# Updating the sample retention states in the feed-forward stage instead of the mixer

## The chip, the core and the metric

The kernel runs on one core of a Trainium2 chip. The core has several engines that work side by side and wait for each other by semaphores: PE (matrix products; PEld is its loading of stationary operands), DVE (elementwise, two operands), ACT (elementwise, one operand, with functions), POOL, and SP, which here only issues DMA transfers, in order. Times are microseconds (us) on the device. The metric is the time of one execution, the median over several runs.

## The reference

One decoder layer for 256 prompt positions and 8 samples of 8 new positions each (320 columns N in the kernel; D_MODEL is 2048). The inputs' norm feeds one projection, whose columns go to an S5 mixer (a diagonal state-space scan) and to retention with 8 heads of width 128. Their outputs are joined, projected and added; a SwiGLU feed-forward part (D_FF 5632) and a last norm follow. The part that the change touches is the state that retention hands back for the samples:

```
chunk = math.gcd(l, RET_CHUNK)                  # 8 for a sample: one chunk
k_decay = exp(log_gamma[:, None] * (chunk - 1.0 - idx))
r_new = r * chunk_decay + einsum('bhmd,bhme->bhde', kc * k_decay, vc)
```

For each of 8 heads and 8 samples `r_new` is a 128x128 matrix: the old one (input `state_ret`, in the kernel `r0[h]`, 512 KB per head) times a constant, plus the product of 8 decayed keys with 8 values. It is an output (`rs_o[h]`, 512 KB per head) and nothing later in the layer reads it. The old state is also read by the attention of the same head.

## The kernel before

The weights, some 210 MB, are streamed once. `wload` fetches tiles of 128x1024 (512 KB) on SP's queue into `raw`, ACT casts them to `hi` (fp32r, the one-pass format), and DVE forms the rest, `lo = raw - hi`. `gemm` then makes each product of a weight tile in three one-pass matmuls (L136 to L138: hi by hi, hi by lo, lo by hi) of 320 columns. The weights' tiles rotate through a pool `wp` with three buffers for each of `raw`, `hi` and `lo`. From the first `up` gemm of the feed-forward stage on, the loads use a second pool, `wp2`, with four, three and three.

The stages follow each other: up to 421 us the mixer (all columns of `w_in`, with the heads and the S5 chunks woven in), up to 563 us the output projections (`w_out`, `w_glu`, `w_out`), then the feed-forward stage: `ffn_in` with eleven pairs of gemms, gate and up, for each quarter of D_FF, and `ffn_out`.

PE's and POOL's orders are written by hand. A planner's clock `clk` adds an assumed cost for each matmul, and generators (`head_k`, `head_v`, the S5 chunks) yield delays from the table `DL`; when one is due, `run_due` puts its next burst of small matmuls between two matmul triples of the running gemm. DVE's, ACT's and SP's orders come from a scheduler with priorities. SP's queue is in order: a load whose buffer isn't free holds back all the loads behind it.

For each head, `do_q` loads `r0[h]` into `rt` (one buffer); `head_k` transposes the keys (`pst`), scales them (`kd`, ACT, L628) and makes the scores (`pss`); `head_v` does the values (`vT`), spreads the sample's values by a block mask over four samples (`vb`, POOL, L650), and makes the output `po`, reading `rt`. Last comes `update` (L707 to L717), due `DL["u"]` later. The keys and values of the samples lie at partitions 64 to 127, 32 of them for each group of four samples. The two products `psu` are plain fp32 matmuls with 32 rows of contraction and 512 columns, in the PSUM pair "misc", which `pst`, `pss`, `pk` and others share. DVE adds them to the old state in `rt` (scalar_tensor_tensor, shown under its helper's line L175), and SP stores `rt`.

At the feed-forward stage's entry, `hhi` and `hlo` of the last column block and the sum of squares `acc` (DVE) are completed; `ffn_norm` makes the reciprocal root: a matmul `ps_r` sums `acc`, a chain of 11 small DVE operations from `ms` to `ry` computes the root, and a second `ps_r` broadcasts it. ACT copies the result to `rbc2`, which the evictions of the gemms' results read.

Of the kernel before, what the change touches and what calls it, by code (L numbers as in the profile page):

```python
# [12 lines left out]
F32 = mybir.dt.float32  # L13
F32R = mybir.dt.float32r
# [3 lines left out]
ADD, SUB, MUL = ALU.add, ALU.subtract, ALU.mult  # L18
PSUM = bass.MemoryType.PSUM

P = 128
D = 2048
KT = D // P
NP, NB, NS = 256, 8, 8
N = NP + NB * NS
H = 8
# [18 lines left out]
def hybrid_kernel(ctx, tc, xT, w_in, w_out, w_glu, w_fi, w_fo, vecs, s5p, bc, x0,  # L45
# [3 lines left out]
    pe, act, dve, pool, sp = nc.tensor, nc.scalar, nc.vector, nc.gpsimd, nc.sync  # L49

    cst = ctx.enter_context(tc.tile_pool(name="cst", bufs=1))
    wp = ctx.enter_context(tc.tile_pool(name="wp", bufs=1))
    ps_acc = ctx.enter_context(tc.tile_pool(name="ps_acc", bufs=2, space=PSUM))

    def f(t):
        return t.bitcast(F32)
# [4 lines left out]
    ones = cst.tile([P, P], F32, name="ones")  # L61
    pool.memset(ones, 1.0)
    vec = cst.tile([P, vecs.shape[1]], F32, name="vec")
    voff = {}
    o = 0
    for nm, n in (("g_mix", 16), ("g_ffn", 16), ("g_fin", 16), ("d", 8), ("bglu", 8), ("gn", 8)):
# [7 lines left out]
    class Clk:  # L74
        now = 0.0
        n = 0
# [19 lines left out]
    def mm(cost, *a, **k):  # L96
        pe.matmul(*a, **k)
        clk.now += cost
# [71 lines left out]
    def tt(out, a, b, op):  # L170
        dve.tensor_tensor(out, a, b, op)  # L171
        return out

    def stt(out, a, s, b, o1, o2):
        dve.scalar_tensor_tensor(out, a, s, b, o1, o2)  # L175
        return out
# [48 lines left out]
    mp = retpool.enter_context(tc.tile_pool(name="mp", bufs=1, side="right"))  # L225
# [7 lines left out]
    def misc(name):  # L233
        return ps_m.tile([P, 512], F32, name=name, tag="misc", bufs=2)
# [4 lines left out]
    rtok = mp.tile([P, 3], F32, name="rtok")  # L239
    csr = mp.tile([P, 2, N], F32, name="csr")  # L240
    kdc = mp.tile([P, H, 3], F32, name="kdc")
    bmk = mp.tile([P, 4], F32, name="bmk")
    gqt = mp.tile([P, H, NS], F32, name="gqt")
    retp = mp.tile([P, H, N], F32, name="retp")

# [357 lines left out]
    GAM = [1.0 - 2.0 ** (-5.0 - h) for h in range(H)]  # L603
# [17 lines left out]
    def head_k(h, q_, qg, k_, R):  # L621
        yield DL["k"]
        pst = misc("pst")
        for i, s in enumerate(STARTS):
            tr(pst[:, P * i:P * i + P], k_[:, s:s + P])
        kd = mp.tile([P, 3, P], F32, name="kd", tag="kd", bufs=1)
        for i in range(3):
            act.mul(kd[:, i], pst[:, P * i:P * i + P], kdc[:, h, i:i + 1])  # L628
        pss = misc("pss")
        mm(0.43, pss[:, 0:256], k_[:, 0:P], q_[:, 0:256], start=True, stop=True)  # L630
        mm(0.22, pss[:, 256:384], k_[:, P:256], q_[:, P:256], start=True, stop=True)
        mm(0.22, pss[:, 384:448], k_[:, 192:320], q_[:, 256:320], start=True, stop=True)
        sm = mp.tile([P, 384], F32, name="sm", tag="sm", bufs=1)
        mk = R["mk"]
        tt(sm[:, 0:256], pss[:, 0:256], mk[:, 0:NP], MUL)
        tt(sm[:, 256:384], pss[:, 256:384], mk[:, 0:P], MUL)
        tt(smp[64:128, :, 0:NS], pss[64:128, 384:448].rearrange("p (b t) -> p b t", t=NS),
           mk[64:128, NP:320].rearrange("p (b t) -> p b t", t=NS), MUL)
        R["kd"], R["sm"] = kd, sm

    def head_v(h, v_, qg, rt, R):
        yield DL["v"]
        pst2 = misc("pst2")
        for i, s in enumerate(STARTS):
            tr(pst2[:, P * i:P * i + P], v_[:, s:s + P])
        vT = mp.tile([P, 3, P], F32, name="vT", tag="vT", bufs=1)
        for i in range(3):
            act.mul(vT[:, i], pst2[:, P * i:P * i + P], rtok[:, i:i + 1])
        vb = mp.tile([P, 4, P], F32, name="vb", tag="vb", bufs=1)
        pool.tensor_tensor(vb[64:128], vT[64:128, 2].unsqueeze(1).to_broadcast([64, 4, P]),  # L650
                           bmk[64:128].unsqueeze(2).to_broadcast([64, 4, P]), MUL)
        yield DL["o"]
        kd, sm = R["kd"], R["sm"]

        po = ps_v.tile([P, 4, P], F32, name="po", tag="po", bufs=1)
        mm(0.22, po[:, 0], sm[:, 0:P], vT[:, 0], start=True, stop=True)
        mm(0.22, po[:, 1], sm[:, P:256], vT[:, 0], start=True, stop=False)
        mm(0.22, po[:, 1], sm[:, 256:384], vT[:, 1], start=False, stop=True)

        for g in range(2):  # L660
            mm(0.22, po[:, 2 + g], smp[:, 4 * g:4 * g + 4].rearrange("p b t -> p (b t)"), vT[:, 2],
               start=g == 0, stop=False, skip_group_check=True)
        for g in range(2):
            for j in range(4):
                mm(0.06, po[32 * j:32 * j + 32, 2 + g], qg[:, 4 * g + j], rt[:, 4 * g + j], start=False,
                   stop=True, tile_position=(0, 32 * j), skip_group_check=True)
        st = mp.tile([P, 4, 6], F32, name="st", tag="st", bufs=1)
        mv = mp.tile([P, 2, 4], F32, name="mv", tag="mv", bufs=1)
        y = mp.tile([P, 2, 4], F32, name="gy", tag="gy", bufs=1)
        with tc.high_priority(offset=GN):  # L670
            for i in range(4):
                dve.bn_stats(st[:, i], po[:, i])
                dve.bn_aggr(mv[:, :, i], st[:, i])
            ts(mv[:, 1], mv[:, 1], -0.5, MUL, -0.5 * EPS, ADD)
            rsqrt(mv[:, 1], y[:, 0], y[:, 1])
            stt(y[:, 1], mv[:, 0], -1.0, y[:, 0], MUL, MUL)
        on = mp.tile([P, 4, P], F32, name="on", tag="on", bufs=1)
        for i in range(4):
            act.activation(on[:, i], po[:, i], AF.Identity, scale=y[:, 0, i:i + 1],
                           bias=y[:, 1, i:i + 1])  # L680
        psr = misc("psr")
        mm(0.22, psr[:, :P], kd[:, 0], vT[:, 0], start=True, stop=False)
        mm(0.22, psr[:, :P], kd[:, 1], vT[:, 1], start=False, stop=True)
        rp = mp.tile([P, P], F32, name="rp", tag="rp", bufs=1)
        act.copy(rp, psr[:, :P])
        sp.dma_start(rp_o[h], rp)
        yield DL["c"]
        pn = misc("pn")
        for i in range(4):
            tr(pn[:, P * i:P * i + P], on[:, i])  # L690
        pairs_ = ((pn[:, 0:NP], retp[:, h, 0:NP], slice(0, NP)),
                  (pn[:, NP:].rearrange("p (b t) -> p b t", t=32)[:, :, 0:NS],
                   retp[:, h, NP:].rearrange("p (b t) -> p b t", t=NS), slice(NP, N)))
        sg = R.get("sgt")
        for i_, o, sl in pairs_:
            if sg is None:
                act.mul(o, i_, v("gn", h))
            else:
                g_ = sg[:, sl]
                if sl.start:  # L700
                    g_ = g_.rearrange("p (b t) -> p b t", t=NS)
                stt(o, i_, v("gn", h), g_, MUL, MUL)
        R["gn"] = True
        if sg is not None:
            R["sg"] = True
        yield from update(h, kd, vb, rt)

    def update(h, kd, vb, rt):
        yield DL["u"]
        psu = [misc("psu") for _ in range(2)]  # L710
        for i in range(2):
            r = slice(64 + 32 * i, 96 + 32 * i)
            mm(0.43, psu[i], kd[r, 2], vb[r], start=True, stop=True, tile_position=(64 + 32 * i, 0))
        for i in range(2):
            rv = rt[:, 4 * i:4 * i + 4]
            stt(rv, rv, float(GAM[h] ** NS), psu[i].rearrange("p (b e) -> p b e", e=P), MUL, ADD)
        sp.dma_start(rs_o[h], rt)  # L717

    def proj(i):
        return gemm("ps_p", w_in[i], KT, xhi, xlo)  # L720
# [53 lines left out]
    def do_g(h):  # L774
        ps = proj(11 + 4 * h)
        sg = mp.tile([P, N], F32, name="sg", tag="sg", bufs=2)
        with tc.high_priority(offset=EVAC):
# [6 lines left out]
    DL = dict(b1=14.2, k1=2.2, b2=4.6, scan=15.6, x=2.2, k=5.5, v=6.1,  # L784
              o=2.2, u=6.0, c=10.0, n2=1.6, n2b=2.4, nm=7.8)
# [225 lines left out]
    def norm_ps(name):  # L1011
        return ps_n.tile([P, 512], F32, name=name, tag="n", bufs=2)

    def ffn_norm():
# [2 lines left out]
        yield DL["n2b"]  # L1017
        act.copy(rbc2, next(rg))

    def ffn_in(c):  # L1020
        ahi = fp.tile([P, FCT, N], F32R, name="ahi", tag="ahi", bufs=2)
        alo = fp.tile([P, FCT, N], F32R, name="alo", tag="alo", bufs=2)
        for i in range(FCT):
            n = c * FCT + i
            if n == 0:
                spawn(ffn_norm(), DL["n2"])
            pg = gemm("ps_fg", w_fi[2 * n], KT, hhi, hlo)
            g = fp.tile([P, N], F32, name="fg", tag="fg", bufs=2)
            tt(g, pg, rbc2, MUL)
            act.activation(g, g, AF.Silu)  # L1030
            if n == 0:
                wpool[:] = [wp2, WP2]
            pu = gemm("ps_fu", w_fi[2 * n + 1], KT, hhi, hlo)
            u = fp.tile([P, N], F32, name="fu", tag="fu", bufs=2)
            tt(u, pu, rbc2, MUL)
            tt(u, u, g, MUL)
            act.copy(ahi[:, i], u)
            tt(alo[:, i], u, f(ahi[:, i]), SUB)
        return ahi, alo

    wp2 = ctx.enter_context(tc.tile_pool(name="wp2", bufs=1, reuse_waits="tile"))
# [133 lines left out]
```

## Time and profile before

| | |
|---|---|
| runs | 1510.04, 1511.94, 1514.68 us; median 1511.94 |
| profiled execution | 1513.66 us, its span 1510.0 us |
| mean granted clock of PE | 0.987 |
| busy | PE 98%, DVE 57%, ACT 40%, POOL 5% |
| moved by DMA | 224.49 MB, 149 GB/s in the mean |

The span goes from the first to the last instruction on the core; the execution's own time is 3.7 us longer. The granted clock is the share of TensorE's full speed that the chip allowed; 0.5 is 1.2 GHz, 1.0 is 2.4 GHz. Idle time of an engine counts only where the engine that sets the end waits for it.

### The profile page before, as it was taken

How to read it: one execution, taken by the hardware profiler on the slowest of the kernel's cores; microseconds unless marked ns; L12 is line 12 of the kernel's file. 1: busy time of each engine (PE TensorE's matmuls, PEld its weight loads, DVE VectorE, ACT ScalarE, POOL GpSimd, SP SyncE). 2: the span in 40 equal slices, each digit the busy share in tenths (PEclk: the TensorE clock that was granted, in tenths of full speed). 3: DMA queues.
4: the chain of work that ended last, by engine and by line, in shares of the span. 5: the costliest groups of instructions: out<-in, count | busy, mean ns of one | idle time of the engine just before them, and what ended most of it. 6: DMA issues, size and time to landing. Idle time of an engine off the chain costs nothing.

```text
span 1510.0 us, 26190 instructions
## 1 busy us (share of the span) xinstructions
PE 1478.7 (98%) x10574; PEld 1450.5 (96%) x10574; DVE 864.6 (57%) x1490; ACT 608.9 (40%) x971; POOL 80.3 (5%) x167
## 2 busy tenths in 40 slices
PE   8989999999999999999999999999999999999997
PEld 8989899898999999999999999999999999999996
DVE  7988767776755675444454444444444444444454
ACT  6545445454434553333333333333333333333352
POOL 1331310300000000000000000000000000000001
PEclk9999999999999999999999999999999999999998
DMA  8344334333364444444444445544444544445443
GB/s 274 126 149 144 131 112 148 120 123 119 129 230 149 148 164 145 149 154 149 147 152 153 137 135 152 177 145 150 145 133 150 173 153 146 148 129 148 147 153 108
DMA packets 77832, 224.49 MB, mean 149 GB/s; under 512 B 14865, under 2 KB 27281, under 8 KB 77713
## 3 DMA queue, kind: packets, MB, share of 16 engines
q1 hardware_dynamic: 77568, 222.79, 45.6%
q8 instruction: 83, 1.36, 0.4%
q14 instruction: 37, 0.30, 0.1%
q10 hardware_dynamic: 144, 0.04, 0.0%
HBM read 213.85 MB, written 7.63 MB: 147 GB/s over the span
## 4 chain that ended last, share of the span: by engine, by line
PE 67%; DVE 0%; ACT 0%; DVEq 0%; issue 0%
PE ps_fg L136 7%; PE ps_fo L136 7%; PE ps_fo L137 7%; PE ps_fu L137 7%; PE ps_fg L137 7%; PE ps_fu L136 7%; PE ps_fg L138 7%; PE ps_fu L138 7%; PE ps_fo L138 7%; PE ps_o L137 1%; PE ps_o L138 1%; PE ps_o L136 1%; PE ps_g L137 1%; PE ps_g L138 1%; PE ps_g L136 1%; DVE x L171 0%
## 5 line engine op out<-in xcount | busy, mean ns | idle before, releaser
L126 DVE TENSOR_TENSOR lo<-raw,hi 128x1024 fp32r<-128x1024 f32 (+1 forms) x420 | 472.2, 1125 | 416.1 <-ACT hi L125 415.8
L125 ACT CAST hi<-raw 128x1024 fp32r<-128x1024 f32 (+1 forms) x420 | 406.4, 968 | 742.5 <-PE ps_fo L137 189.3
L136 PE MATMUL ps_fo<-ahi,hi 128*128 128x320 f32 x704 | 217.5, 309 | 0.0
L137 PE MATMUL ps_fo<-alo,hi 128*128 128x320 f32 x704 | 217.5, 309 | 0.0
L136 PE MATMUL ps_fg<-hhi,hi 128*128 128x320 f32 x704 | 217.5, 309 | 0.0
L138 PE MATMUL ps_fo<-ahi,lo 128*128 128x320 f32 x704 | 217.5, 309 | 0.0
L138 PE MATMUL ps_fg<-hhi,lo 128*128 128x320 f32 x704 | 217.4, 309 | 0.0
L137 PE MATMUL ps_fg<-hlo,hi 128*128 128x320 f32 x704 | 217.4, 309 | 0.0
L137 PE MATMUL ps_fu<-hlo,hi 128*128 128x320 f32 x704 | 217.4, 309 | 0.0
L136 PE MATMUL ps_fu<-hhi,hi 128*128 128x320 f32 x704 | 217.4, 309 | 0.0
L138 PE MATMUL ps_fu<-hhi,lo 128*128 128x320 f32 x704 | 217.4, 309 | 0.0
L136 PE MATMUL ps_p<-xhi,hi 128*128 128x320 f32 x576 | 187.8, 326 | 0.0
L137 PE MATMUL ps_p<-xlo,hi 128*128 128x320 f32 x576 | 181.3, 315 | 0.0
L138 PE MATMUL ps_p<-xhi,lo 128*128 128x320 f32 x576 | 181.1, 314 | 0.0
L137 PEld LDWEIGHTS ps_fg<-hlo,hi 128*128 128x128 f32 x704 | 132.4, 188 | 0.0
L136 PEld LDWEIGHTS ps_fo<-ahi,hi 128*128 128x128 f32 x704 | 132.4, 188 | 0.0
L136 PEld LDWEIGHTS ps_fg<-hhi,hi 128*128 128x128 f32 x704 | 132.4, 188 | 0.0
L136 PEld LDWEIGHTS ps_fu<-hhi,hi 128*128 128x128 f32 x704 | 132.4, 188 | 0.0
L137 PEld LDWEIGHTS ps_fu<-hlo,hi 128*128 128x128 f32 x704 | 132.4, 188 | 0.0
L138 PEld LDWEIGHTS ps_fo<-ahi,lo 128*128 128x128 f32 x704 | 132.4, 188 | 0.0
L138 PEld LDWEIGHTS ps_fu<-hhi,lo 128*128 128x128 f32 x704 | 132.4, 188 | 0.0
L138 PEld LDWEIGHTS ps_fg<-hhi,lo 128*128 128x128 f32 x704 | 132.3, 188 | 0.0
(407 smaller groups left out, 2008.3 us busy)
## 6 DMA issues: line engine op xcount, KB each, us to landing
raw<-w_fi SPq DMA_DIRECT2D x176, 512.0 KB, 3.6
raw<-w_in SPq DMA_DIRECT2D x76, 512.0 KB, 3.7
raw<-w_fo SPq DMA_DIRECT2D x64, 512.0 KB, 3.6
raw<-w_out SPq DMA_DIRECT2D x32, 512.0 KB, 3.7
raw<-w_fo SPq DMA_DIRECT2D x64, 192.0 KB, 2.4
rt<-r SPq DMA_DIRECT2D x8, 512.0 KB, 3.7
rs_o<-rt SPq DMA_DIRECT2D x8, 512.0 KB, 3.5
raw<-w_glu SPq DMA_DIRECT2D x8, 512.0 KB, 3.6
```

The lines of the kernel that those rows point to most:

```text
L125: act.copy(hi[:, :m], raw[:, :m])
L126: dve.tensor_tensor(lo[:, :m], raw[:, :m], f(hi[:, :m]), SUB)
L136: pe.matmul(ps, hi, xhi[:, k], start=k == 0, stop=False)
L137: pe.matmul(ps, hi, xlo[:, k], start=False, stop=False)
L138: pe.matmul(ps, lo, xhi[:, k], start=False, stop=k == nk - 1)
```

## The change

The matrices `kd` and `vb` of the samples are no longer used in the mixer. `head_k` and `head_v` put the samples' scaled keys and values of each head, 64 rows each, into one tile `kv` (64 values rows at partitions 0 to 63, keys at 64 to 127), and `update` is gone, its store of `rt` too. In `ffn_in(0)`, after the first pair of gemms, `states_split` casts all of `kv` to `hi` and forms the rest `lo`, and 16 copies from SBUF to SBUF build two stationary and two moving tiles in which four groups of 32 partitions hold high and low parts: keys (hi, hi, lo, lo) against values (hi, lo, hi, lo). One matmul with 128 rows so sums all four partial products. After pairs 2 to 9 `states_load` fetches `r0[h]` a second time and DVE spreads the values by the block mask (two operations of 128x512); after pairs 3 to 10 `states_add` does two matmuls, two DVE additions and the store for one head. The buffers are those of `wp`, which the weights no longer use by then, and the PSUM pair of the norms.

```diff
-        kd = mp.tile([P, 3, P], F32, name="kd", tag="kd", bufs=1)
-        for i in range(3):
+        kd = mp.tile([P, 2, P], F32, name="kd", tag="kd", bufs=1)
+        for i in range(2):
             act.mul(kd[:, i], pst[:, P * i:P * i + P], kdc[:, h, i:i + 1])
+        act.mul(kv[64:128, h], pst[64:128, 2 * P:3 * P], kdc[64:128, h, 2:3])
...
-        vb = mp.tile([P, 4, P], F32, name="vb", tag="vb", bufs=1)
-        pool.tensor_tensor(vb[64:128], vT[64:128, 2].unsqueeze(1).to_broadcast([64, 4, P]),
-                           bmk[64:128].unsqueeze(2).to_broadcast([64, 4, P]), MUL)
+        act.copy(kv[0:64, h], vT[64:128, 2])
...
-        yield from update(h, kd, vb, rt)
-
-    def update(h, kd, vb, rt):
-        yield DL["u"]
-        psu = [misc("psu") for _ in range(2)]
-        for i in range(2):
-            r = slice(64 + 32 * i, 96 + 32 * i)
-            mm(0.43, psu[i], kd[r, 2], vb[r], start=True, stop=True, tile_position=(64 + 32 * i, 0))
-        for i in range(2):
-            rv = rt[:, 4 * i:4 * i + 4]
-            stt(rv, rv, float(GAM[h] ** NS), psu[i].rearrange("p (b e) -> p b e", e=P), MUL, ADD)
-        sp.dma_start(rs_o[h], rt)
...
+    def states_split():
+        kvh, kvl = (wp.tile([P, 8, P], F32R, name=n, tag=n, bufs=3) for n in ("hi", "lo"))
+        act.copy(kvh, kv)
+        tt(kvl, kv, f(kvh), SUB)
+        SU["k"] = [wp.tile([P, 8, P], F32R, name="hi", tag="hi", bufs=3) for _ in range(2)]
+        SU["v"] = [wp.tile([P, 8, P], F32R, name="lo", tag="lo", bufs=3) for _ in range(2)]
+        for i in range(2):
+            for a in range(4):
+                d = slice(32 * a, 32 * a + 32)
+                sp.dma_start(f(SU["k"][i][d]), f((kvh, kvl)[a // 2][64 + 32 * i:96 + 32 * i]))
+                sp.dma_start(f(SU["v"][i][d]), f((kvh, kvl)[a % 2][32 * i:32 * i + 32]))
+
+    def states_load(h):
+        rt = wp.tile([P, NB, P], F32, name="raw", tag="raw", bufs=3)
+        sp.dma_start(rt, r0[h])
+        n = ("hi", "lo")[h % 2]
+        vm = wp.tile([P, NB, P], F32R, name=n, tag=n, bufs=3)
+        for i in range(2):
+            tt(vm[:, 4 * i:4 * i + 4], f(SU["v"][i][:, h]).unsqueeze(1).to_broadcast([P, 4, P]),
+               bmk.unsqueeze(2).to_broadcast([P, 4, P]), MUL)
+        SU[h] = rt, vm
+
+    def states_add(h):
+        rt, vm = SU.pop(h)
+        for i in range(2):
+            q = slice(4 * i, 4 * i + 4)
+            ps = norm_ps("psu")
+            pe.matmul(ps, SU["k"][i][:, h], vm[:, q].rearrange("p b e -> p (b e)"), start=True, stop=True)
+            stt(rt[:, q], rt[:, q], float(GAM[h] ** NS), ps.rearrange("p (b e) -> p b e", e=P), MUL, ADD)
+        sp.dma_start(rs_o[h], rt)
...
@@ in ffn_in, after each pair i
+            if c == 0:
+                if i == 0:
+                    states_split()
+                if 3 <= i:
+                    states_add(i - 3)
+                if 2 <= i < 2 + H:
+                    states_load(i - 2)
```

SP's queue at the turn to the feed-forward stage, before: 88 loads of `w_fi` stand in a row behind those of `w_out`.

```order
L124 DMA raw<-w_glu 128x1024 x8
L124 DMA raw<-w_out 128x1024 x16
L124 DMA raw<-w_fi 128x1024 x88
L124 DMA raw<-w_fo 128x1024
L124 DMA raw<-w_fo 128x384
```

The same place after:

```order
L127 DMA raw<-w_out 128x1024 x16
L127 DMA raw<-w_fi 128x1024 x2
L1028 DMA raw<-r 128x1024 x3
L127 DMA raw<-w_fi 128x1024 x7
L1023 DMA hi<-hi 32x1024
L1024 DMA lo<-hi 32x1024
L127 DMA raw<-w_fi 128x1024
L1023 DMA hi<-hi 32x1024
L1024 DMA lo<-lo 32x1024
L127 DMA raw<-w_fi 128x1024
```

Three loads of `r` stand between the second and the third load of `w_fi`, and the first copies come behind the ninth.

DVE at the same turn, before: the end of the chain that makes the reciprocal root (`ry` the last of it, L175), and the splits of the next `w_fi` tiles (L126).

```order
L171 TENSOR_TENSOR rt<-ry 128x3
L171 TENSOR_TENSOR rt<-rt,ms 128x3
L175 SCALAR_TENSOR_TENSOR ry<-rt,ry 128x3
L126 TENSOR_TENSOR lo<-raw,hi 128x1024 x3
L171 TENSOR_TENSOR fg<-ps_fg,rbc_5946 128x320
```

The same place after:

```order
L174 TENSOR_TENSOR rt<-ry 128x3
L129 TENSOR_TENSOR lo<-raw,hi 128x1024
L174 TENSOR_TENSOR rt<-rt,ms 128x3
L178 SCALAR_TENSOR_TENSOR ry<-rt,ry 128x3
L129 TENSOR_TENSOR lo<-raw,hi 128x1024 x2
L174 TENSOR_TENSOR fg<-ps_fg,rbc_5883 128x320
```

The split of the third `w_fi` tile stands inside the root's chain instead of behind it. Some rows earlier, the split of `kv` (`lo<-kv,hi`) has come ahead of the last `hlo` and `acc`; ACT's cast `hi<-kv` stands ahead of the last `hhi`.

PE in the mixer where the first head's update lay, before: the two `psu` between gemm triples, then one triple, then `pk`, which belongs to the S5 tables.

```order
L136 MATMUL ps_p<-xhi,hi 128x320
L137 MATMUL ps_p<-xlo,hi 128x320
L138 MATMUL ps_p<-xhi,lo 128x320
L97 MATMUL psu<-vb,kd 128x512 x2
L136 MATMUL ps_p<-xhi,hi 128x320
L137 MATMUL ps_p<-xlo,hi 128x320
L138 MATMUL ps_p<-xhi,lo 128x320
L97 MATMUL pk__1164<-cl_130,bl 32x128 x8
```

The same place after:

```order
L139 MATMUL ps_p<-xhi,hi 128x320
L140 MATMUL ps_p<-xlo,hi 128x320
L141 MATMUL ps_p<-xhi,lo 128x320
L100 MATMUL pk__1163<-cl_131,bl 32x128 x8
L139 MATMUL ps_p<-xhi,hi 128x320
```

No `psu` is left between the gemms, and `pk` comes 18 gemm matmuls behind the burst ahead of it, where it came twelve and the two `psu` behind it.

## Rows read from the trace of the kernel before

**Rows 1.** The page: the span, and busy time of each engine.

```profile
span 1510.0 us, 26190 instructions
PE 1478.7 (98%) x10574; PEld 1450.5 (96%) x10574; DVE 864.6 (57%) x1490; ACT 608.9 (40%) x971; POOL 80.3 (5%) x167
```

**Rows 2.** Windows (engines, PEclk, DMA share, GB/s) of the stages.

```profile
50.00:421.00 371.00, 355.66 (x2961) 331.68 (x2960) 278.82 (x635) 175.61 (x398) 70.83 (x144) 0.96 0.40 130
421.00:563.00 142.00, 141.41 (x963) 140.89 (x963) 89.14 (x130) 67.58 (x100) 0.00 (x0) 1.00 0.54 176
555.00:560.00 5.00, 5.00 (x36) 5.00 (x35) 3.56 (x7) 2.25 (x4) 0.00 (x0) 1.00 0.82 266
600.00:650.00 50.00, 50.00 (x343) 50.00 (x342) 23.76 (x29) 18.27 (x22) 0.00 (x0) 1.00 0.45 151
```

**Rows 3.** Groups by line and form: idle time before them stands behind the bar.

```profile
L97 PE MATMUL psu<-vb,kd 32*128 32x512 f32 x32 | 12.9, 670 | 2.9 <-DVE retp L175 2.2 <-DVE rt L175 0.8
L175 DVE SCALAR_TENSOR_TENSOR rt<-rt,psu 128x512 f32<-128x512 f32 x16 | 10.5, 679 | 2.3 <-PE psu L97 2.3
```

**Rows 4.** PE waits: total, times, longest, in us.

```profile
PE pst L102 <- DVE rt L175: 2.5, 1, 2.5
PE pn L102 <- ACT on L679: 2.5, 2, 2.0
PE pk__1164 L97 <- DVE rt L175: 2.4, 1, 2.4
PE psu L97 <- DVE retp L175: 2.2, 1, 2.2
PE pss L97 <- ACT kd L628: 1.0, 1, 1.0
```

**Rows 5.** Windows of line 136 alone, four stretches at half clock.

```profile
88.03:91.44 3.41, 2.04 (x4) 1.34 (x5) 0.50 0.69 267
183.61:190.44 6.83, 2.92 (x6) 1.94 (x6) 0.50 0.47 164
340.62:347.45 6.83, 1.84 (x4) 1.32 (x4) 0.50 0.47 161
384.99:388.40 3.41, 1.99 (x5) 1.36 (x5) 0.50 0.74 276
```

**Rows 6.** Timeline of PE, gemm matmuls at half clock.

```profile
88.71 0.47 PE L137 MATMUL ps_p<-xlo,hi 128*128 128x320 f32 x1
88.98 0.47 PE L138 MATMUL ps_p<-xhi,lo 128*128 128x320 f32 x1
```

**Rows 7.** Timeline of PE, matmuls of 512 columns behind the last gemm.

```profile
1494.59 0.96 PE L111 MATMUL warm_ps<-ones 128*128 128x512 f32 x3
1495.97 2.33 PE L111 MATMUL warm_ps<-ones 128*128 128x512 f32 x9
```

**Rows 8.** Timeline of DVE, ACT and PE as the feed-forward stage begins.

```profile
560.70 1.23 DVE L126 TENSOR_TENSOR lo<-raw,hi 128x1024 fp32r<-128x1024 f32 x1 [0.44 <-ACT hi L125]
564.41 0.55 DVE L175 SCALAR_TENSOR_TENSOR hlo<-x,vec,hhi 128x320 fp32r<-128x320 f32 x1 [0.63 <-ACT hhi L995]
566.34 0.16 DVE L167 TENSOR_SCALAR ms<-ps_r 128x3 f32<-128x3 f32 x1 [0.98 <-PE ps_r L97]
568.31 0.16 DVE L175 SCALAR_TENSOR_TENSOR ry<-rt,ry 128x3 f32<-128x3 f32 x1
564.64 1.98 ACT L125 CAST hi<-raw 128x1024 fp32r<-128x1024 f32 x2
569.33 0.83 PE L97 MATMUL ps_r<-ident,ry 128*128 128x128 f32 x6
```

**Rows 9.** DMA issues of 551.3 to 554.2 us, and its last two; median us to landing.

```profile
raw<-w_fi SPq DMA_DIRECT2D x5, 512.0 KB, 7.9
raw<-w_fi SPq DMA_DIRECT2D x2, 512.0 KB, 9.1
```

**Rows 10.** DMA issues of the whole span, small copies from SBUF to SBUF.

```profile
kst<-up__941 SPq DMA_DIRECT2D x16, 10.0 KB, 2.7
```

More of the change, by code (lines that the diff above doesn't have):

```diff
@@ L63, in hybrid_kernel @@
     vec = cst.tile([P, vecs.shape[1]], F32, name="vec")
+    bmk = cst.tile([P, 4], F32, name="bmk")
+    kv = cst.tile([P, H, P], F32, name="kv")
     voff = {}
@@ L241, in hybrid_kernel @@
     kdc = mp.tile([P, H, 3], F32, name="kdc")
-    bmk = mp.tile([P, 4], F32, name="bmk")
     gqt = mp.tile([P, H, NS], F32, name="gqt")
@@ L1018, in ffn_norm @@
         act.copy(rbc2, next(rg))
+    SU = {}
+    def states_split():
[26 more added lines that the diff above has]
+        sp.dma_start(rs_o[h], rt)
     def ffn_in(c):
```

## The prediction, made before the changed kernel had run

> **What bounds the kernel now.** I read the page first [rows 1]: PE is busy for 98% of the span, so time can only be won where PE does less or waits less. Then the windows by stage [rows 2]. In the output projections (421 to 563 us) and in the feed-forward stage PE has no idle time: 963 matmuls in 142.00 us, 0.147 us each. In the mixer (50 to 421 us) PE is busy for 355.66 of 371.00 us, its mean granted clock is 0.96, and DVE is busy for 278.82 us. So the mixer alone holds idle PE time, 15.3 us, and some of its busy time is spent at half clock. The list of PE's waits [rows 4] says what ends the idle time: in the five entries shown it is DVE three times and ACT twice, and two of DVE's are `rt`, the update's own product. The feed-forward stage is PE and nothing else; whatever is added to PE there is paid in full, and whatever is added to DVE (23.76 of 50 us) or DMA (share 0.45) is paid only if it becomes late.
>
> **What leaves the mixer.** First the matmuls. The group of `psu` matmuls [rows 3] is busy for 12.9 us and has 2.9 us of idle time ahead of it: 15.8 us of PE time. Its 16 products of 512 columns show as 32 records, two for each, since they are plain fp32. Second, the waits on what the update leaves behind it [rows 4]: `pk__1164` 2.4 us and `pst` 2.5 us both stand in the shared "misc" PSUM pair until DVE has done with `psu` (releaser `rt`, L175), and `pss` waits 1.0 us for `kd`, which comes late because that `pst` was late. Together 5.9 us. Third, the clock. Four stretches follow directly on these waits or on the update's wait of 2.2 us (187 us) and of 0.8 us (384 us): there the granted clock is 0.50, that is 1.2 GHz instead of 2.4 [rows 5], and PE had just stood idle. Their gemm matmuls start 0.27 us apart [rows 6] against 0.147. The window rows of line 136, the first of each three, count 4, 6, 4 and 5 of them, 19 in all, so 57 gemm matmuls at 0.12 us too much: 6.8 us. The most that the mixer can give up is 15.8 + 5.9 + 6.8 = **28.5 us**.
>
> **What of that comes back.** DVE loses 16 evictions of 0.679 us [rows 3], 10.9 us, but stays 72% busy (268 of 371), and the burst that took 1.6 us of PE's time per head (12.9/8) also gave DVE that much time to catch up. The other bursts now lie elsewhere between the gemms (the `yield` of the update and its cost of 0.86 on the planner's clock are gone). Where each will wait, no row of before can tell. Bounds: nothing comes back, or everything. The nearest row is `pn`, which waits for ACT, has nothing to do with the update, and stands 2.0 us at the longest [rows 4]. I take two such waits, one of them at the mixer's end, where the last head's rest now runs into the output projection, each with a half-clock stretch of a mean 1.7 us (6.8/4): 7.4 us. The mixer then gives 28.5 - 7.4 = 21.1 us. POOL's product `vb` goes too; POOL is busy for 80.3 us of the span and nothing waits for it, so I put that at nothing; ACT's additional copies into `kv` (eight, smaller than a `kd` product) lie in its idle half of the mixer and count nothing, and would cost PE at most their own time if the `pst` chain ran over them.
>
> **What the feed-forward stage pays on PE.** 16 one-pass products of 128x512 are added, 128 rows deep. The nearest rows are the warm-up matmuls of that size in the tail [rows 7]: nine take 2.33 us, three 0.96, so six more take 1.37, 0.228 us each. 16 x 0.228 = **3.7 us**. They have one operand in common and the added ones do not, so this is rather the floor; the half-clock price, twice as much, is the ceiling. The Trainium skill, "TensorE: Matmul & The Clock Gate", section "Back-to-back issue gap", gives 131 ns for a sustained matmul of 512 columns; by that the 16 would be 2.1 us and the sum 1.6 us lower. The row says 228 ns, and the row decides.
>
> **What its entry pays.** This is the part that speaks against the change. Before, SP issues 88 loads of `w_fi` in a row, and the third tile, t2, is among the five issued in 551.3 to 554.2 us [rows 9], over 15 us before ACT and DVE are done with it. After, three loads of `r` stand ahead of t2 in SP's queue, and they take raw buffers of the small pool, of which the third comes free when DVE has split tile t1: 560.70 + 1.23 = 561.93 us [rows 8]. SP runs in order, so t2 is issued no sooner, together with its three followers and the last `r` loads. Five loads issued close together took 7.9 us to land [rows 9]: t2 lands at 569.8. ACT's cast takes 1.05 us or a little less (two in 1.98 us, [rows 8]), DVE's split 1.23 us: 572.1. DVE's order has this split inside the chain of small operations that makes the reciprocal root, ahead of its last two (0.2 us apart), so the root is there at 572.5 instead of 568.5, and PE's broadcast matmul `ps_r`, which started at 569.33, can start at 572.5: **3.2 us** later. In that time the split of `kv` is hidden: it stands ahead of the last `hlo` and delays `acc` by its 1.23 us less the 0.63 that DVE waited there, with the wait for its own ACT cast some 0.9 us, which the wait for t2 swallows. PE idles for up to 2.3 us at one place (3.2 less 0.9), about as long as the waits after which the clock fell in the mixer, so I add one half-clock stretch, 1.7 us: 4.9 in all. Bounds: if t2 lands early, the sum is the 0.9 of the split of `kv`, then t2's split in the chain, 1.23, less the 0.86 us between the chain's end (568.47) and 569.33: 1.3 us. If t2 lands like the last two of those loads, 9.1 us, it is 4.4 + 1.7 = 6.1 us.
>
> **What the stage hides.** Per pair of gemms (14.1 us at 48 x 2 matmuls) DVE gets two mask products and two evictions of 128x512, 2.7 us, and goes from 23.8 to about 33 of 50 us. Each pair also moves 1 MB more (a load and a store of 512 KB), 74 GB/s on top of 151; 266 GB/s were moved in 555 to 560 us [rows 2]. I put both at nothing. If that cover went, a wait of DVE's 2.7 us per pair would cost up to 21 us; the rows leave a third of the engine free.
>
> **The sum.** -28.5 + 7.4 + 3.7 + 4.9 = -12.5 us. Of the profiled execution's 1513.66 us that leaves 1501.2. This execution lies 1.72 us over the median of the runs, 1511.94, against which the result is told: **1499.5 us**.
>
> **The rivals.**
> 1. *The whole prize is kept.* The moved bursts find their inputs ready, t2 comes early. -28.5 + 3.7 + 1.3 = -23.5: 1488.4 us. For it: all the waits taken out have the update's buffers as cause. Against it: DVE at 72%, and t2 behind three loads.
> 2. *The mixer is paced by DVE.* Then only DVE's 10.9 us are won there: -10.9 + 3.7 + 4.9 = -2.3, 1509.6 us; with the dear entry (6.1) 1510.8. For it: all of the long waits but one go back to DVE; against: DVE idles for 92 us there.
> 3. *Slower: the mixer keeps its length.* Every burst waits for the last step of its own chain (rotation, `kd`, scan), PE's saved matmuls become idle time, and the feed-forward stage's 8.6 us are the whole effect: 1520.5 us. It decides where the mixer gives less than 4.1 us. For it: other bursts have waits of their own (`pn`, [rows 4]); against: eight bursts of 1.6 us on an engine that is 96% busy.
> 4. *Slower: the copies block the loads.* Sixteen copies of 32 partitions stand in SP's queue between the next fourteen or so loads of `w_fi`, some 28 us in which the transfers need a share of 0.45, 12.6 us. If each copy held all transfers for the 2.7 us that a far smaller one takes to land [rows 10], 43 us were added and 28 us fall short: 1527. Slower from 2.0 us each ((28 - 12.6 + 12.5 + 4.5) / 16). For it: nothing in before copies 128 KB between 32 partitions. Against: five loads were under way at once [rows 9], which a blocked queue doesn't show. The Trainium skill, "DMA: Bandwidth & Descriptors", section "Rules for kernel authors", says that transfers to separate parts of the partitions serialize and should be one; it speaks for this rival, and no run here shows it so far.
>
> **How the numbers follow.** Forecast, 1494 to 1506: 0.54. Rival 1 (below 1494): 0.18. Rival 2 (1506 to 1512): 0.18. Rivals 3 and 4: 0.06 and 0.04. The range goes from rival 1's floor to rival 2's dear end, 1488 to 1511, and leaves out the slower cases and some 0.05 at either end: 0.8 inside. A change under 0.3%, 4.5 us, can't be told from none here: faster is below 1507.4, which is the forecast, rival 1 and a quarter of rival 2: 0.77. Same takes most of the rest of rival 2 and the mild end of rival 3: 0.15. Slower 0.08.
>
> **What the profile after would show.** Right, if the mixer's 371 us shrink by some 21 (the first output projection starting near 400 instead of 421), the granted clock there is above 0.96, no `psu` appears before the feed-forward stage, `ps_r` there waits for DVE for 2 to 3 us with t2's split late behind its DMA, and from 580 us on PE is busy without a gap but for 16 matmuls of about 0.23 us. Wrong, if new PE waits of over 2 us stand in the mixer on operations other than the update's (rivals 2, 3), if the entry wait exceeds 5 us, or if gaps on PE appear in the feed-forward stage while copies are under way (rival 4).

## The result and the profile after

The changed kernel takes 1491.28 us (median of 4 runs, 1490.19 to 1493.44) against 1510.99 us, 19.7 us less; the ratio is 0.9868, interval 0.9846 to 0.9889. The forecast was 12.5 us less. The profiled execution took 1490.19 us. Its span and busy times on the page answer to [rows 1]:

```profile
span 1488.4 us, 26179 instructions
PE 1462.0 (98%) x10558; PEld 1443.7 (97%) x10558; DVE 865.4 (58%) x1507; ACT 615.1 (41%) x980; POOL 77.1 (5%) x159
```

The same three stages by windows (columns as in [rows 2]: the mixer, the output projections, 50 us of the feed-forward stage):

```profile
50.00:393.60 343.60, 333.80 (x2933) 320.29 (x2932) 259.17 (x616) 179.61 (x405) 67.65 (x136) 1.00 0.40 128
393.60:536.00 142.40, 141.40 (x963) 140.88 (x962) 90.74 (x135) 68.11 (x102) 0.00 (x0) 1.00 0.52 169
600.00:650.00 50.00, 50.00 (x340) 49.75 (x339) 30.50 (x40) 16.95 (x22) 0.00 (x0) 1.00 0.69 223
```

The mixer still has the same gemms, but PE's idle time in it fell from 15.3 to 9.8 us (333.80 of 343.60 us busy), its clock is now 1.00, and it ends 27 us earlier. The projections are as long as before. In the feed-forward stage DVE went from 23.76 to 30.50 of 50 us and DMA from 151 to 223 GB/s, and PE is still busy throughout.

Where the 21.6 us between the two spans lie is read best from landmarks. The groups by tile give, for the third matmul line of each gemm, the first and the last start (in us, behind the three durations). Before:

```profile
L138 PE MATMUL ps_fg<-hhi,lo x704: 307/309/314, 563.4 to 1331.9; 128*128 128x320 f32 x176
L138 PE MATMUL ps_fu<-hhi,lo x704: 307/308/310, 572.1 to 1339.0; 128*128 128x320 f32 x176
L138 PE MATMUL ps_fo<-ahi,lo x704: 305/309/310, 874.8 to 1493.9; 128*128 128x320 f32 x176
```

After:

```profile
L141 PE MATMUL ps_fg<-hhi,lo x704: 303/309/310, 536.2 to 1309.7; 128*128 128x320 f32 x176
L141 PE MATMUL ps_fu<-hhi,lo x704: 306/308/312, 546.2 to 1316.8; 128*128 128x320 f32 x176
L141 PE MATMUL ps_fo<-ahi,lo x704: 305/309/309, 852.6 to 1471.6; 128*128 128x320 f32 x176
```

Up to `ps_fg` the kernel gained 563.4 - 536.2 = 27.2 us. From `ps_fg` to `ps_fu`, the entry, it lost 10.0 - 8.7 = 1.3. From `ps_fu` to the last `ps_fo` it lost 925.4 - 921.8 = 3.6, and behind it, to the end of the span, 0.7. Sum: -21.6. (The two profiled executions lie toward opposite ends of their runs, hence 21.6 of span beside 19.7 of the medians.) From this `ps_fg` to the end of the span it is 1510.0 - 563.4 = 946.6 us before and 1488.4 - 536.2 = 952.2 after, so the feed-forward half costs 5.6 us in all.

The list of PE's waits in the mixer after (total, times, longest), which answers to [rows 4]:

```profile
PE pn L105 <- ACT on L680: 3.9, 4, 1.3
PE pt L105 <- DVE retp L178: 1.4, 1, 1.4
PE pst L105 <- DVE cl L174: 1.4, 1, 1.4
PE pk__1163 L100 <- DVE cl L174: 1.2, 1, 1.2
```

No entry for the update is left, as it must be; and none of the others is longer than 1.4 us, where four of before lasted 2.0 us or more.

The entry, on DVE:

```profile
533.54 1.23 DVE L129 TENSOR_TENSOR lo<-raw,hi 128x1024 fp32r<-128x1024 f32 x1 [0.45 <-ACT hi L128]
537.05 1.23 DVE L174 TENSOR_TENSOR lo<-kv,hi 128x1024 fp32r<-128x1024 f32 x1 [0.44 <-ACT hi L1016]
541.79 1.22 DVE L129 TENSOR_TENSOR lo<-raw,hi 128x1024 fp32r<-128x1024 f32 x1
543.12 0.16 DVE L178 SCALAR_TENSOR_TENSOR ry<-rt,ry 128x3 f32<-128x3 f32 x1
```

On ACT, the cast of t2:

```profile
540.49 1.05 ACT L128 CAST hi<-raw 128x1024 fp32r<-128x1024 f32 x1 [2.64 <-DMA raw<-w_fi]
```

And on PE:

```profile
539.29 0.80 PE L100 MATMUL ps_r<-ones,acc 128*128 128x1 f32 x6 [1.02 <-DVE acc L174]
543.34 0.93 PE L100 MATMUL ps_r<-ident,ry 128*128 128x128 f32 x6
```

The order is as forecast: t1's split ends at 534.77, and only then can SP issue t2 behind the loads of `r`; ACT waits 2.64 us for its landing; its split stands in the root's chain, just ahead of the last two steps. But t2 was there at 540.5, 5.7 us after 534.77 and not 7.9, and the chain had not got that far: DVE waits for t2's cast nowhere. PE waits only the 1.02 us for `acc`, behind the split of `kv`.

Two of the added products and the gemm behind them:

```profile
595.15 0.63 PE L1041 MATMUL psu<-hi 128*128 128x512 f32 x2
595.61 0.31 PE L139 MATMUL ps_fg<-hhi,hi 128*128 128x320 f32 x1
```

0.46 us for two, 0.23 each, at the tail's price [rows 7].

### The profile page after: what moved, and what is told of

Read it like the earlier page. It is cut to its first block, busy times and chain, and to the rows that moved or that the text cites. A ratio compares the mean times of both kernels' runs of the same rounds, so it can differ in the third digit from the quotient of the medians.

```text
span 1488.4 us, 26179 instructions
## 1 busy us (share of the span) xinstructions
PE 1462.0 (98%) x10558; PEld 1443.7 (97%) x10558; DVE 865.4 (58%) x1507; ACT 615.1 (41%) x980; POOL 77.1 (5%) x159
## 4 chain that ended last, share of the span: by engine, by line
PE 68%; DVE 1%; ACT 0%; issue 0%; DVEq 0%
PE ps_fo L139 7%; PE ps_fu L139 7%; PE ps_fu L141 7%; PE ps_fo L140 7%; PE ps_fu L140 7%; PE ps_fo L141 7%; PE ps_fg L139 7%; PE ps_fg L141 7%; PE ps_fg L140 7%; PE ps_o L139 1%; PE ps_o L140 1%; PE ps_o L141 1%; PE ps_g L140 1%; PE ps_g L141 1%; PE ps_g L139 1%; DVE x L174 0%
## 5 line engine op out<-in xcount | busy, mean ns | idle before, releaser
L139 PE MATMUL ps_p<-xhi,hi 128*128 128x320 f32 x576 | 183.6, 319 | 0.0
L141 PE MATMUL ps_p<-xhi,lo 128*128 128x320 f32 x576 | 177.9, 309 | 0.0
L140 PE MATMUL ps_p<-xlo,hi 128*128 128x320 f32 x576 | 177.8, 309 | 0.0
```

The costliest lines, as they stand in the source:

```text
L139: pe.matmul(ps, hi, xhi[:, k], start=k == 0, stop=False)
L140: pe.matmul(ps, hi, xlo[:, k], start=False, stop=False)
L141: pe.matmul(ps, lo, xhi[:, k], start=False, stop=k == nk - 1)
```

## The experiments

**The mixer's half alone.** The call of the three new functions in `ffn_in` is gone; the old states are stored behind `po`.

```diff
+        sp.dma_start(rs_o[h], rt)
-            if c == 0:
-                if i == 0:
-                    states_split()
...
```

> The mixer's half alone: head_k and head_v as after the change, no update anywhere; the old states are stored unchanged (rs_o from rt, right behind po), so the sample states are not updated. Theory: the mixer won 27 us and the feed-forward half costs 3.6 us for 16 products and 1.3 us at its entry, so this kernel takes 1491.3 - 4.9 = 1486.4 us, and ps_fg starts near 536 us. Rival: the feed-forward half costs the 8.6 us of the forecast somewhere that the landmarks don't show; then 1482.7.

Measured: 1485.85 us, ratio 0.9837 (0.9823 to 0.9852). The first hi-by-lo `ps_fg` starts at 536.8 us, `ps_fu` 8.7 us later. The theory's 1486.4 holds; the feed-forward half costs 5.4 us, not 8.6. The landmarks agree: from the first `ps_fg` to the end of the span this kernel takes 1483.4 - 536.8 = 946.6 us, as before.

**The feed-forward half alone.** The mixer of before with its update, plus the three functions and two ACT copies per head into `kv`.

```diff
         act.mul(kd[:, i], pst[:, P * i:P * i + P], kdc[:, h, i:i + 1])
+        act.copy(kv[64:128, h], kd[64:128, 2])
...
         stt(rv, rv, float(GAM[h] ** NS), psu[i].rearrange("p (b e) -> p b e", e=P), MUL, ADD)
-        sp.dma_start(rs_o[h], rt)
...
+            if c == 0:
+                if i == 0:
+                    states_split()
...
```

> The feed-forward half alone: the mixer of before with its update, whose store is left out, and two more ACT copies per head into kv; states_split, states_load and states_add as after the change, and they store the result. Theory: 1511.0 + 4.9 = 1515.9 us, with the waits and half-clock stretches of the mixer as before. Rival (the feed-forward half costs 8.6): 1519.6.

Measured: 1514.55 us, ratio 1.0031 (1.0015 to 1.0048), so 2.3 to 7.3 us more; the entry is 10.0 us (571.0 - 561.0). That takes in the theory's 4.9, and leaves out the rival's 8.6. The two halves add up: -24.9 and +3.8 make -21.1 beside the measured -19.7, within what the runs scatter.

From the first `ps_fg` (561.0) to the end of the span (1513.2) this kernel takes 952.2 us, as the changed one does. But it reaches `ps_fg` 2.4 us sooner than the profiled execution of before, although products and additions of the update are both in place: `pk` waits 0.9 us for `rt` here, 2.4 there. Whether the ACT copies or chance did that is not shown. So gains of the mixer that are read from single traces are good to some 2 us; what lies behind `ps_fg` repeats within 0.1 us.

**PE's order of before, less the products.** The end of each head still waits and is charged on the planner's clock.

```diff
             R["sg"] = True
+        yield DL["u"]
+        clk.now += 0.86
```

> The changed kernel, but the planner still waits DL[u] and charges 0.86 at the end of each head: PE's order in the mixer is that of before, with the psu products taken out and nothing else moved. Theory (the prize is the update's own products, waits and half-clock stretches, wherever the other bursts lie): 1491 us within 3. Rival (the new places of the other bursts won the part that I had not forecast, some 6 us): 1497 or more, with PE waits of 2 us on other operations and half-clock stretches behind them.

Measured: 1485.4 us, ratio 0.9832 (0.9816 to 0.9847). Neither: the changed kernel's new places for the other bursts don't win, they lose. `ps_fg` starts at 531.7 us, 4.5 us before that of the changed kernel, and from there on the two are alike. PE's waits in the mixer:

```profile
PE pt L105 <- DVE retp L178: 1.4, 1, 1.4
PE pst L105 <- DVE cl L174: 1.4, 1, 1.4
PE pk__1157 L100 <- POOL tab L478: 1.2, 1, 1.2
PE pk__1157 L100 <- DVE cl L174: 1.2, 1, 1.2
PE pn L105 <- ACT on L680: 0.5, 1, 0.5
```

Against the changed kernel `pn` on ACT fell from 3.9 us (four times) to 0.5, and small waits on `r4b`, `bst` and `kbd` shrank or went; 1.2 us on POOL's `tab` came in. So the update's departure is worth 563.4 - 531.7 = 31.7 us in the mixer (29.3 against the 561.0 of the feed-forward half alone), and the planner gave 4.5 of them back by moving `pn`, `pk` and others. The medians say 5.9 (1491.28 - 1485.4). Both mixers stand again in kernels further down: with the new places `ps_fg` starts at 536.3 and 538.0 us there, with the old ones at 532.4 and 530.1. So the sign is sure, and the size is 4 to 6 us.

**Which part of the update held PE?** Two kernels on the base of before, with PE's order of before. The first keeps the products and leaves out DVE's additions:

```diff
         for i in range(2):
-            rv = rt[:, 4 * i:4 * i + 4]
-            stt(rv, rv, float(GAM[h] ** NS), psu[i].rearrange("p (b e) -> p b e", e=P), MUL, ADD)
```

> The kernel before with DVE's additions left out: the psu products stay where they are, nobody reads them, and the old states are stored unchanged (the sample states are not updated). Theory (the waits and half-clock stretches come from PSUM buffers that DVE had still to read, and from DVE's 10.9 us): the products' own 12.9 us stay, the waits on rt (2.4 + 2.5 + 0.8), the one of kd behind them and the half-clock stretches at 88, 341 and 385 us go, so 10 to 16 us of the mixer are won: 1495 to 1501. Rival (the prize is the products' own PE time): 1506 or more, with the clock of the mixer as before, 0.96.

Measured: 1495.63 us, ratio 0.9906 (0.9891 to 0.9921), 14.7 us less, inside the theory's span. The window of the mixer and two of its waits:

```profile
50.00:400.00 350.00, 341.61 (x2937) 320.01 (x2936) 267.49 (x618) 175.25 (x398) 70.95 (x144) 1.00 0.43 135
```

```profile
PE pn L102 <- ACT on L679: 2.5, 2, 2.0
PE pt L102 <- DVE retp L175: 1.6, 1, 1.6
```

The clock is 1.00 with all products in place; the waits on `rt` are gone, and those of `pn` and `pt`, which don't belong to the update, stand as before.

The second leaves out the products and keeps the additions, from SBUF:

```diff
-            mm(0.43, psu[i], kd[r, 2], vb[r], start=True, stop=True, tile_position=(64 + 32 * i, 0))
+            clk.now += 0.43
...
-            stt(rv, rv, float(GAM[h] ** NS), psu[i].rearrange("p (b e) -> p b e", e=P), MUL, ADD)
+            stt(rv, rv, float(GAM[h] ** NS), rt[:, 4 - 4 * i:8 - 4 * i], MUL, ADD)
```

> The kernel before with the psu products left out and DVE's additions kept: they add another half of rt from SBUF, so they hold no PSUM buffer (the sample states come out different); the planner's clock is charged as before, so PE's order is that of before without psu. Theory of PSUM buffers held: everything but DVE's time goes, which does not bound the mixer, so up to 30 us are won: 1481 to 1487. Rival (DVE's 10.9 us of additions themselves make the bursts wait): only the products' 12.9 and their waits of 2.9 are won, 1495, and waits of 2 us and half-clock stretches stay on operations behind the additions.

Measured: 1483.63 us, ratio 0.9831 (0.9816 to 0.9845), 26.7 us less: the theory's span. Its longest waits in the mixer:

```profile
PE pt L102 <- ACT bst L531: 2.3, 1, 2.3
PE pst L102 <- DVE cl L171: 1.4, 1, 1.4
PE pn L102 <- ACT bst L531: 1.3, 2, 1.0
PE pt L102 <- DVE bl L171: 1.1, 1, 1.1
```

None is on `rt`, although DVE still does all 16 additions. A 2.3 us wait on ACT has come in, though, with a stretch at 0.50 from 84.0 to 90.8 us, so the additions' time may not be quite free. The first hi-by-lo `ps_fg` without additions, without products, and without both (the order experiment):

```profile
L138 PE MATMUL ps_fg<-hhi,lo x704: 303/309/312, 546.4 to 1314.9; 128*128 128x320 f32 x176
L138 PE MATMUL ps_fg<-hhi,lo x704: 307/309/311, 538.5 to 1307.1; 128*128 128x320 f32 x176
L141 PE MATMUL ps_fg<-hhi,lo x704: 303/309/312, 531.7 to 1305.2; 128*128 128x320 f32 x176
```

Against the 563.4 of before that is -17.0, -24.9 and -31.7. The two parts alone would make -41.9; some 10 us are in both, the time that needs a product and a late addition at once. (The profiled execution without products is the slowest of its four, 1487.08 us. The medians give -14.7, -26.7 and, with the feed-forward half's 5.6 us added to the order experiment's 25.4, -31.0: again some 10 us.) I read them as the waits for a PSUM pair that PE can't have back before DVE has read it, with the half-clock stretches behind them.

**The entry.** The first three loads of `r` and the split of `kv` wait for a later pair, by a one-column write into their buffers.

```diff
+        tt(kvh[:, 0, 0:1], u[:, 0:1], u[:, 0:1], MUL)
         act.copy(kvh, kv)
...
+        if h < 3:
+            tt(rt[:, 0, 0:1], u[:, 0:1], u[:, 0:1], MUL)
         sp.dma_start(rt, r0[h])
```

> The changed kernel with the split of kv and the first three loads of r made to wait for the end of a later pair of gemms (a one-column DVE write into the same buffer ahead of each): SP's queue has eleven w_fi loads in a row again, the root's chain on DVE is whole and the split of kv is no longer ahead of acc. Theory: the 1.3 us of the entry go, 1490.0 us, and the wait of 1.0 us of ps_r for acc is gone from the list; the difference is too small for the timing, so the landmark decides (ps_fu starts 8.7 us behind ps_fg as before, instead of 9.95). Rival (the later copies and loads collide with the weights): slower than 1491.3, with gaps on PE between 560 and 620 us.

Measured: 1499.47 us, ratio 0.9929 (0.991 to 0.9947). The entry is mended, 545.0 - 536.3 = 8.7 us, and the wait for `acc` is gone, but 10.6 us are lost later: `ps_fu` to the last `ps_fo` takes 936.0 us instead of 925.4. PE's waits between 530 and 720 us, with a stretch at 0.50 behind them (597.3 to 607.5 us):

```profile
PE psu L1044 <- DVE hi L174: 4.7, 1, 4.7
PE psu L1044 <- issue: 2.9, 1, 2.9
```

DVE's two mask products for head 0, each ahead of a `psu`; the second waits for the last copy:

```profile
596.26 0.68 DVE L174 TENSOR_TENSOR hi<-lo,bmk 128x512 fp32r<-128x512 f32 x1
601.52 0.69 DVE L174 TENSOR_TENSOR hi<-lo,bmk 128x512 fp32r<-128x512 f32 x1 [4.10 <-DMA lo<-lo]
```

The last kind of copy, four issues, first and last start (here, and then in the changed kernel):

```profile
L1025 SPq DMA_DIRECT2D lo<-lo x4: 507/508/581, 561.6 to 596.7; - x4
```

```profile
L1024 SPq DMA_DIRECT2D lo<-lo x4: 507/544/584, 553.4 to 588.0; - x4
```

The 2.9 us ahead of the first product the profile puts down to nothing. They ended with DVE's first mask product: it ends at 596.94, and PE starts at 597.04. That mask product had no idle time of DVE ahead of it; in the changed kernel the same operation waited for a copy `lo<-hi`, and the last copy of that kind landed at 594.1 here. Whether the copy or DVE's order held it is not shown. The transfers are not slow (4.4 to 4.6 us to landing at the median of each kind). They stand one by one between loads of `w_fi` in SP's queue, and from 565 us on they are issued some 3.5 us apart, since the loads wait for buffers (14 times between 550 and 600 us, 34.1 us in all); so the row of copies, begun later, ends 9 us later, and the second product is 4.7 us too early for it. That is the rival's place, but by the queue, not by colliding transfers. In the changed kernel the last copy was issued at 588.0 and the first product stands at 595.15.

**The products twice.**

```diff
-            pe.matmul(ps, SU["k"][i][:, h], vm[:, q].rearrange("p b e -> p (b e)"), start=True, stop=True)
+            for j in range(2):
+                pe.matmul(ps, SU["k"][i][:, h], vm[:, q].rearrange("p b e -> p (b e)"), start=j == 0, stop=j == 1)
```

> The changed kernel with each of the 16 products of the feed-forward stage done twice into the same PSUM bank (the update comes out twice as large). If they are paid in full at the tail's price, 0.228 us each, 3.6 us are added: 1494.9, and ps_fu to ps_fo grows by as much. Rival (by the two operands that change from product to product they cost more, or less where the array takes them in stream): 0.131 us each gives 1493.4, 0.39 us (the duration that the profile shows for one) 1497.5.

Measured: 1495.02 us, 3.7 us over the changed kernel; `ps_fu` to the last `ps_fo` grew from 925.4 to 929.2 us. Four products, and the gemm behind them:

```profile
597.00 1.09 PE L1042 MATMUL psu<-hi 128*128 128x512 f32 x4
597.93 0.30 PE L139 MATMUL ps_fg<-hhi,hi 128*128 128x320 f32 x1
```

0.93 us for four, 0.23 each again: paid in full, at the tail's price.

**The entry mended, on the faster order.** The loads of `r` wait as above; only the second half of `kv`'s split waits, for the root's copy; the products come one pair later, the last two heads' together.

```diff
         act.copy(kvh, kv)
+        tt(kvl[:, 0, 0:1], rbc2[:, 0:1], rbc2[:, 0:1], MUL)
         tt(kvl, kv, f(kvh), SUB)
...
-                if 3 <= i:
-                    states_add(i - 3)
+                if 4 <= i:
+                    states_add(i - 4)
...
+                if i == FCT - 1:
+                    states_add(H - 1)
```

> e3_order with the entry mended: the first three loads of r wait for the third pair of gemms, the second half of the split of kv waits for the copy of the root, and the products come one pair later (the last two heads' both behind the last pair). Theory: the 1.3 us of the entry go without a wait for the copies, 1484.1 us, ps_fu 8.7 us behind ps_fg, no wait of PE on psu. Rival (as in e6_entry the later copies are not done when the first product comes): 1487 or more, with PE waiting at psu.

Measured: 1488.7 us, ratio 0.9858 (0.9844 to 0.9873), slower than the order experiment. PE waits from the entry on:

```profile
PE psu L1046 <- DVE raw L178: 2.3, 2, 1.6
PE ps_r L100 <- DVE acc L174: 0.3, 1, 0.3
```

The entry took 541.3 - 532.4 = 8.9 us, as wanted, and no copy is late; but the last two heads' four products now follow each other, and the third and the fourth must wait, 0.7 and 1.6 us, until DVE has read an earlier one out of the PSUM pair (`raw`, L178). A stretch at 0.50 from 695.0 us on comes with it.

**The last products spread.**

```diff
+            if n == FCT - 1:
+                states_add(H - 2)
             pu = gemm("ps_fu", w_fi[2 * n + 1], KT, hhi, hlo)
...
-                if 4 <= i:
+                if 4 <= i < FCT - 1:
```

> e8_late with the last products spread: head 6 between the gate and the up gemm of the last pair, head 7 behind it, so that two products no longer follow on two whose PSUM pair DVE has still to read. Theory: the 2.3 us of waits at psu and the half-clock stretch of 1.2 us behind them go; with the mended entry 1484.3 us, 1.1 below e3_order. Rival (the moved loads or copies delay something else): a wait of PE between 530 and 720 us stays, and 1486 or more.

Measured: 1483.95 us (5 runs), ratio 0.982 (0.9801 to 0.984). All waits of PE from the entry on:

```profile
PE ps_r L100 <- DVE acc L174: 0.3, 1, 0.3
```

This is the fastest of the kernels that compute everything: some 7 us less than the changed one, most of it by the order, a good 1 us by the entry. The last of these is under what timing alone can show; it rests on the landmarks and on the list of waits. The entry took 539.0 - 530.1 = 8.9 us against 10.0, and from the first `ps_fg` to the end of the span it is 951.1 us against 952.2 in the order experiment.

## Why the prediction was right, and where its sizes were off

The measured 1491.28 us lies inside the range, 8.2 us below the forecast of 1499.5. It is in the span that I gave to rival 1 (below 1494, 0.18) and not in the forecast's own (1494 to 1506, 0.54). The mechanism held, and the sizes that were off all erred to the same side. By the landmarks the sum is -31.7 + 4.5 + 3.6 + 1.3 + 0.7 = -21.6, where I had -28.5 + 7.4 + 3.7 + 4.9 = -12.5.

- *What bounds the kernel.* Right: the mixer was the one place with time to win. The feed-forward stage paid for PE's added products and, beyond them, only at its entry and 0.7 us at its end.
- *What leaves the mixer, at most 28.5 us.* Too low: 31.7 us went when nothing else was moved, or 29.3 by the other trace with the update in it, so 1 to 3 us are missing. They are most likely `pn`'s wait on ACT (2.0 us) with its half-clock stretch at 283 us, which I had left out; I had called it foreign to the update, but with additions and products both gone it fell to 0.5 us. Without the additions alone it stayed at 2.0, without the products alone its longest was 0.6. What held it was not taken apart further.
- *What comes back, 7.4 us.* The mechanism was right, and the term was mis-sized. The moved bursts do wait more, and it cost 4.5 us (4 to 6), shown by the kernel with the old order. But those waits were at most 1.4 us, and in the profiled execution no half-clock stretch with gemm work followed on them, whereas I had charged two. Counted from my ceiling of 28.5, only 1.3 came back.
- *The products, 3.7 us.* Right: 3.6 by the landmarks, 3.7 by doubling. The Trainium skill's 131 ns ("TensorE: Matmul & The Clock Gate", "Back-to-back issue gap") was not reached; the rows say 0.23 us.
- *The entry, 4.9 us.* Right in the order of things, wrong in size: 1.3 us, my lower bound, made of its very terms (the split of `kv` 0.9, t2's split 1.2, less the 0.86 us in hand). I had taken the 7.9 us of five loads issued together; t2 came in 5.7, so DVE was never late for it and PE's idle time stayed at 1.02 us (I had named 2 to 3), without a fall of the clock.
- *What the stage hides.* Right: no wait of PE between 545 and 720 us. The 0.7 us behind the last `ps_fo` had no term of mine: 16.1 us to the end of the span before and with the mixer's half alone, 16.8 after. Their cause stays open.
- *The rivals.* The whole prize kept (1488.4) came nearest, 2.9 us off. Its early t2 was right, but that the moved bursts find their inputs ready was not; a larger prize, less what came back, made 27.2 us beside its 28.5, which is luck. The pacing by DVE is refuted: with all of DVE's additions left in, the mixer still gave 24.9 us. The mixer that keeps its length is refuted by the landmarks. The copies that block the loads: not in the changed kernel. From the DMA issues between 520 and 620 us there, the weights' loads and the copies, with the median to landing last:

```profile
raw<-w_fi SPq DMA_DIRECT2D x29, 512.0 KB, 4.6
hi<-hi SPq DMA_DIRECT2D x4, 128.0 KB, 5.5
lo<-hi SPq DMA_DIRECT2D x4, 128.0 KB, 5.8
lo<-lo SPq DMA_DIRECT2D x4, 128.0 KB, 4.4
hi<-lo SPq DMA_DIRECT2D x4, 128.0 KB, 4.6
```

A load takes 4.6 us against 3.6 on the page of before (the loads and stores of the states are under way there, too), a copy 4.4 to 5.8, and PE waits for neither. The Trainium skill, "DMA: Bandwidth & Descriptors", "Rules for kernel authors", advises against splitting a transfer over two halves of the partitions, since the two serialize; here the copies did not hold up the loads so far that anything waited, and what the delayed kernel paid came by the order of SP's queue.

## What to carry to other kernels

A small product whose PSUM buffer waits for a busy engine costs far more than its matmuls: here 12.9 us of matmuls held 29 to 32 us, through the waits of whatever needs the pair next and the half clock behind them; so look at who waits for the eviction. When work is taken out of an order written by a planner's clock, try first with the clock's charge left in: the removal and the shift of everything else are two changes, and here the second cost 4 to 6 us. Where copies stand between loads in an in-order queue, their pace is that of the loads' buffers, not of the transfers.

## What the runs showed of the hardware

Leaving out DVE's additions alone, with all of the products in place, raised the mixer's granted clock from 0.96 to 1.00. Idle times of PE of 2.0 to 2.5 us in the mixer before came with a stretch at 0.50. In the mixer after, single ones of up to 1.4 us did not, but two shorter ones close together did. After, on PE's timeline:

```profile
346.37 0.33 PE L105 MATMUL pn<-ident,on 128*128 128x128 f32 x1 [1.29 <-ACT on L680]
347.66 0.33 PE L105 MATMUL pn<-ident,on 128*128 128x128 f32 x1 [0.97 <-ACT on L680]
```

and the window behind them:

```profile
348.44:351.85 3.41, 3.41 (x69) 2.96 (x70) 0.61 (x2) 0.68 (x2) 0.00 (x0) 0.50 0.44 154
```

That stretch cost little only because no gemm matmul, just small ones, lay in it. So it is not the single longest wait of a list that tells of the clock. Before, a stretch at 0.50 (384.99 us, [rows 5]) came 1.8 us behind an idle time of only 0.8 us.

Nor does the same wait tell it twice. The 1.4 us of `pst` at 56 us, which no fall followed in the changed kernel, stood ahead of one in the entry experiment, whose mixer is the same:

```profile
56.03 0.52 PE L105 MATMUL pst<-ident,k__768 128*128 128x128 f32 x3 [1.42 <-DVE cl L174]
```

```profile
57.96:61.37 3.41, 3.41 (x16) 3.41 (x14) 2.76 (x14) 2.55 (x6) 3.02 (x11) 0.50 0.11 25
```

In the order experiment two waits of 1.19 us, 1.6 us apart, stood ahead of a stretch at 0.50 from 87.1 us on; in the last kernel, which has the mixer of the order experiment, the same two waits (1.20 and 1.19 us) stood ahead of none. A half-clock stretch in one trace thus belongs in part to that execution, and a change should not be credited with a single one.
